# Hybrid attention and SSM layer: later loads, an earlier split and a regrouped frame in the SSM chain

## The chip, the cores and the metric

One core of a Trainium2 chip runs the kernel. The time is that of one execution on the device, in microseconds (us); lower is better. The kernel before took 1496.83 us, the median of three runs (1495.3, 1496.83 and 1497.23).

Five engines run their own instruction streams in order: PE (TensorE, matrix products), DVE (VectorE), ACT (ScalarE), POOL (GpSimd) and SP (which here only issues DMAs). They wait for each other through semaphores. ACT issues DMAs too.

## The reference

One layer over 2048 tokens of width 1024, all in float32. One input projection gives q, k, v, the gate inputs and the SSM input u:

```
h = rms_norm(x); proj = h @ w_in
q, k, v, z_attn, u_ssm, z_ssm, g = split(proj)
attn = windowed_gqa(q, k, v, sink, table) * silu(z_attn)      # 8 heads, window +-128
y = s5_bidirectional(u_ssm, ...)      # 32 groups of 16 channels, 64 complex states,
                                      # a scan over all tokens in both directions
ssm = gelu(y) -> GLU -> * silu(z_ssm)
merged = sigmoid(g_attn) * (attn @ w_a) + sigmoid(g_ssm) * (ssm @ w_s)
out = rms_norm(x + merged @ w_out)
```

The SSM is per group a complex diagonal recurrence x[t] = a x[t-1] + B u[t], y = Re(C x) + D u, forward and backward.

## The kernel before, in words

**Precision.** Each float32 operand of a product is split into a high and a low part (names with h and l at the end: Uh and Ul, Mh and Ml, Hh and Hl). ACT makes the high part, DVE or POOL the low part as the difference. A product is three matmuls: high x high, high x low, low x high.

**Stages.** First u, k and v are projected for the four blocks of 512 tokens. Then come 112 projections of 24 matmuls each (128 columns of w_in, one block of tokens): q, za and zs, then the gate columns g, twice over for two blocks each. Each key of columns serves two projections in a row. Its weights are loaded on SP's queue, their high part is made by ACT (line 163) and their low part by POOL (line 155, four instructions). The result goes from an output bank of PE (three are in turn) to memory through ACT; for za and zs also through DVE (line 401). Beside the projections runs a side chain: first the SSM, then attention, then the preparation of the last stage. GLU, branch and output products follow.

**What sets the order.** The order is written out when the kernel is built. The side chain is a generator. Inside each projection, `turn` is called four times, and each call adds half of a rate to a credit; while the credit is positive, a step of the chain is issued, which costs 1 (half that in attention). RATE2 holds for the SSM and the first part of attention. So a step's instructions stand in each engine's stream behind those of the projections issued until then, whether its engine is by then free or not.

**The SSM chain.** The parameters are computed on DVE beside the first projections. `ssm` then works through 8 frames of 4 groups (half 0 and half 1, two groups each), about 15 steps a frame. In frame i:

- `inject` (line 858) multiplies U, the frame's input, by W into PSUM, and ACT copies it to X; `zmat` (line 821) builds with the output table wo and the input matrix a small matrix Z, which is stored and loaded again as M (`load_m`), 128 wide.
- `rotate` (lines 867 to 870), `scan` (879), `rotate` back, on DVE, half by half.
- `high_h` on ACT and `low_h` on DVE (891) split the states of a half into Hh and Hl; `split_m` (749) gives Mh and Ml.
- `emit(i, half)` (901, 905) on PE adds M x U and ws x H for the half's two groups. ws are the split parts of the table wo.
- For frame i+1, `prep_e` and `prep_w` fill tables on POOL through a list that `slot` empties one by one, `prep_o` the output table wo on DVE (692 to 694), `mats` transposes wt to W on PE (796), `split_u` splits U. `load_u` loads U of frame i+2.

Of the kernel before, what the change touches and what calls it, by code (L numbers as in the profile page):

```python
# [7 lines left out]
F32 = mybir.dt.float32  # L8
# [4 lines left out]
ALU = mybir.AluOpType  # L13
# [10 lines left out]
G, P, C, T = 32, 64, 16, 8  # L24
M = S // T
GB = 4
RATE1 = 1.336
RATEP = 2.6
RATE2 = 1.237
RATE3 = 1.499  # L30
WLAG = 2
WOP = 1
# [5 lines left out]
def kernel(  # L38
# [9 lines left out]
    nc = tc.nc  # L48
    V, A, Q, PE = nc.vector, nc.scalar, nc.gpsimd, nc.tensor
    x = x[0]  # L50
    w_in = w_in[0]
    out = out[0]
# [3 lines left out]
    def scratch(name, shape):  # L56
        if dbg and name in dbg:
            return dbg[name]
        return dram.tile(shape, F32, name=name)

    uS = scratch("uS", [512, T, M])
# [357 lines left out]
    wo_re = prm.tile([128, G, T], F32, name="wo_re")  # L419
    wo_im = prm.tile([128, G, T], F32, name="wo_im")  # L420
# [8 lines left out]
    cc_re = prm.tile([128, G, C], F32, name="cc_re")  # L429
    cc_im = prm.tile([128, G, C], F32, name="cc_im")  # L430
# [238 lines left out]
    def ssm(pool):  # L669
        f, b_ = slice(0, 64), slice(64, 128)  # L670
        st = {}
# [3 lines left out]
        sh = [128, GB, T, C]  # L675

        def bc(t, i, wide):
            return t[:, i * GB:(i + 1) * GB].unsqueeze(3 if wide else 2).to_broadcast(sh)
# [3 lines left out]
        def product(o, p, q, eng):  # L682

            def part(n, a, b, c, d, op, gs):
                if eng is Q:
                    tmp = [pool.tile([128, 2, T, C], F32, tag=f"t{m}", name=f"t{m}") for m in range(2)]
                else:
                    r = rtile().rearrange("p g r m -> p g (r m)")  # L690
                    tmp = [r[:, m].rearrange("p (g j c) -> p g j c", g=GB, c=C) for m in range(2)]
                eng.tensor_tensor(tmp[0], a[:, gs], b[:, gs], ALU.mult)
                eng.tensor_tensor(tmp[1], c[:, gs], d[:, gs], ALU.mult)
                eng.tensor_tensor(o[n][:, gs], tmp[0], tmp[1], op)

            for n, x_ in enumerate(((p[0], q[0], p[1], q[1], ALU.subtract), (p[0], q[1], p[1], q[0], ALU.add))):
                w = 2 if eng is Q else GB
                for g in range(0, o[n].shape[1], w):
                    if eng is Q:
                        work.append(lambda n=n, x_=x_, g=g: part(n, *x_, slice(g, g + w)))  # L700
                    else:
                        part(n, *x_, slice(g, g + w))
# [7 lines left out]
        def slot():  # L710

            count[0] += 1
            if work and (count[0] % 2 == 0 or len(work) > 3):
                work.pop(0)()
            yield

        def rtile():
            return pool.tile([128, 2, 2, M], F32, tag="rt", name="rt")

        def table(o, i, p_re, p_im, q_re, q_im, eng):  # L720
            pr, pi, qr, qi = bc(p_re, i, 1), bc(p_im, i, 1), bc(q_re, i, 0), bc(q_im, i, 0)
            product(o, (pr, pi), (qr, qi), eng)
# [3 lines left out]
            st[i] = {"wt": o}  # L726
            table(o, i, wi_re, wi_im, bb_re, bb_im, eng)

        def prep_o(i, eng=Q):
            raw_o[i] = [pool.tile(sh, F32, tag=f"wo{n}", name=f"wo{n}") for n in range(2)]  # L730
            table(raw_o[i], i, wo_re, wo_im, cc_re, cc_im, eng)

        def prep_e(i, half):

# [8 lines left out]
        def mirror_e(i, half):  # L743
            for n, t in enumerate(ph[i, half]):
                A.activation(t[:, :, 126::-1], t[:, :, 128:255], AF.Copy, scale=1.0 - 2.0 * n)

        def parts(hi, lo, raw):
            A.activation(hi, raw, AF.Copy)
            V.tensor_tensor(lo, raw, hi.bitcast(F32), ALU.subtract)
            return hi, lo  # L750
# [14 lines left out]
        def chan(t, g):  # L765

            return bass.AP(tensor=t.tensor, offset=t.offset + g * C * T * M, ap=[[M, T], [T * M, C], [1, M]])

        def load_u(i, half):
            lo = pool.tile([128, 2, M], F32R, tag=f"U{half}l", name=f"U{half}l", bufs=2)  # L770
            raw = lo.bitcast(F32)
            for j in range(2):
                A.dma_start(out=raw[:, j], in_=chan(uS, i * GB + half * 2 + j))
            raw_u[i, half] = lo, raw

        def split_u(i, half):
            hi = pool.tile([128, 2, M], F32R, tag=f"U{half}h", name=f"U{half}h", bufs=2)
            st[i].setdefault("U", []).append(parts(hi, *raw_u.pop((i, half))))

        def split_m(i):  # L780
            st[i]["M"] = parts(pool.tile([128, GB, 128], F32R, tag="Mh", name="Mh"), *st[i].pop("m"))
# [80 lines left out]
        def rotate(i, half, back):  # L862

            X = st[i]["X"][half][:, :, :, 1:M]
            c, s_ = (t[:, :, 0:M - 1].unsqueeze(2).to_broadcast([128, 2, 2, M - 1]) for t in ph[i, half])
            t = rtile()[:, :, :, 1:M]
            V.tensor_tensor(t, X[:, :, ::-1], s_, ALU.mult)  # L867
            V.tensor_tensor(X, X, c, ALU.mult)
            for r in range(2):
                V.tensor_tensor(X[:, :, r], X[:, :, r], t[:, :, r], ALU.add if r == back else ALU.subtract)  # L870

        def scan(i, half):

            X = st[i]["X"][half]
            for j in range(2):
                g = i * GB + half * 2 + j
                for r in range(2):
                    v = X[:, j, r, 1:M]
                    V.tensor_tensor_scan(v, rho[:, g:g + 1].to_broadcast([128, M - 1]), v, 0.0, ALU.mult, ALU.add)  # L879
# [8 lines left out]
        def low_h(i):  # L888
            H, xs = st[i]["H"]
            for rows, xv in xs:  # L890
                V.tensor_tensor(H[1][rows], xv, H[0][rows].bitcast(F32), ALU.subtract)  # L891
# [21 lines left out]
        def frame(i):  # L913

            nx = i + 1 if i + 1 < NB else None
            nn = i + 2 if i + 2 < NB else None
            ms = mats(nx) if nx else None
            zs = zmat(i)
            inject(i, 0)
            yield from slot()  # L920
            next(zs)
            inject(i, 1)
            yield from slot()
            rotate(i, 0, 0)
            next(zs)
            inject(i, 2)
            yield from slot()
            scan(i, 0)
            next(zs)
            inject(i, 3)  # L930
            if i > 0:
                mirror_e(i, 1)
            yield from slot()
            next(zs, None)
            rotate(i, 0, 1)
            if nx:
                prep_e(nx, 0)
            yield from slot()
            A.dma_start(out=zS[i], in_=st[i].pop("z"))
            if nx:  # L940
                next(ms)
            yield from slot()
            if nx:
                next(ms)
            split_o(i)
            yield from slot()
            load_m(i)
            high_h(i, 0)
            if nx:
                next(ms, None)  # L950
            if nn:
                prep_w(nn)
            yield from slot()
            low_h(i)
            rotate(i, 1, 0)
            yield from slot()
            split_m(i)
            scan(i, 1)
            yield from slot()
            rotate(i, 1, 1)  # L960
            if nx:
                prep_e(nx, 1)
            yield from slot()
            yield from slot()
            yield from emit(i, 0)
            yield from slot()
            high_h(i, 1)
            yield from slot()
            low_h(i)
            if nx:  # L970
                mirror_e(nx, 0)
            yield from slot()
            if nx:
                prep_o(nx, V)
                split_u(nx, 0)
            yield from slot()
            yield from emit(i, 1)
            if nx:
                split_u(nx, 1)
            if nn:  # L980
                load_u(nn, 0)
                load_u(nn, 1)
            st.pop(i)
            yield from slot()

        raw_o, ph = {}, {}
        load_u(0, 0)
        load_u(0, 1)
        prep_w(0, V)
        prep_e(0, 0)  # L990
        prep_e(0, 1)
        drain_work()
        yield
        prep_o(0, V)
        yield
        yield from mats(0)
        split_u(0, 0)
        split_u(0, 1)
        mirror_e(0, 0)
        mirror_e(0, 1)  # L1000
        load_u(1, 0)
        load_u(1, 1)
        prep_w(1)
        yield
        for i in range(NB):
            yield from frame(i)

# [238 lines left out]
    with tc.manual_schedule():  # L1246
# [4 lines left out]
        wo = {}  # L1251
# [80 lines left out]
        for b in range(NBLK):  # L1332
            gen = None
            for i, key in enumerate(wlist):
# [14 lines left out]
                if b == 2 and i == 2:  # L1349
                    pr = add_side(params, RATEP)  # L1350
# [297 lines left out]

        sd = add_side(chain(), RATE2)
        for key in first:  # L1650
# [95 lines left out]
```

## Time and profile before

| | |
|---|---|
| median of the runs | 1496.83 us |
| profiled execution | 1497.58 us |
| its span, first to last instruction | 1495.8 us |
| PE busy | 1411.9 us (94%) |
| DVE busy | 1042.3 us (70%) |
| ACT busy | 659.8 us |
| POOL busy | 636.9 us |
| mean granted clock of PE | 0.981 |

Busy time is the union of an engine's instructions; PE's matmuls overlap, so that one of 128 x 512 lists 0.39 us where the next starts 0.23 us later. A row of a timeline gives start, length, engine, line, operation, result and sources; in brackets stands how long the engine was idle before it and what ended that. The chain of work that ended last is 45% PE and 19% DVE. The SSM frames run from 199 to 660 us, attention from there to about 1045 us.

### The profile page before, as it was taken

What the parts mean: (1) busy time and instruction counts of PE and PEld (TensorE: products, weight loads), DVE (VectorE), ACT (ScalarE), POOL (GpSimd) and SP (SyncE); (2) the same over time, 40 slices, a digit from 0 to 9 for tenths busy, and PEclk for the clock granted to TensorE, in tenths of its full rate; (3) what the DMA queues carried; (4) which work ended last, traced back from release to release, by engine and by line L of the source; (5) the groups of instructions that cost most, each with busy time, mean ns of one, the idle gap of its engine ahead of it and who ended that gap; (6) DMA issues with size and microseconds to landing.
All of it is one profiled execution on the core that took longest, in us unless ns stands there. A gap on an engine that the chain in (4) does not pass through costs nothing.

```text
span 1495.8 us, 19697 instructions
## 1 busy us (share of the span) xinstructions
PE 1411.9 (94%) x6933; PEld 1151.1 (77%) x6933; DVE 1042.3 (70%) x1954; ACT 659.8 (44%) x1213; POOL 636.9 (43%) x683
## 2 busy tenths in 40 slices
PE   7999779899999999899999999999989999999998
PEld 6787567777778777788888888888767887878886
DVE  2427977779788788656999998883678376485442
ACT  6432133433534534535666666664444243243211
POOL 5520187758688787732111111113367054153320
PEclk9999989989999999999999999999999999999999
DMA  8543222322332332455233333334676476375441
GB/s 268 156 105 90 64 81 74 99 92 71 119 106 82 116 106 82 149 170 142 86 95 93 96 95 89 99 99 141 201 210 175 140 185 184 117 186 177 129 120 70
DMA packets 240722, 185.47 MB, mean 124 GB/s; under 512 B 57920, under 2 KB 202432, under 8 KB 240624
## 3 DMA queue, kind: packets, MB, share of 16 engines
q10 hardware_dynamic: 118192, 107.89, 24.5%
q1 hardware_dynamic: 122432, 76.34, 17.1%
q8 instruction: 54, 0.88, 0.2%
q14 instruction: 44, 0.36, 0.1%
HBM read 126.56 MB, written 57.62 MB: 123 GB/s over the span
## 4 chain that ended last, share of the span: by engine, by line
PE 45%; DVE 19%; POOL 7%; DMA 6%; issue 6%; ACT 4%; ACTq 1%; POOLq 0%; DVEq 0%; SPq 0%
PE pj L221 8%; PE pj L220 8%; PE pj L222 8%; PE s L1593 4%; PE s L1592 4%; PE s L1594 4%; POOL wl L155 3%; DMA yt<-yS 2%; PE s L1163 2%; DVE Hl L891 2%; PE s L1110 2%; PE s L1147 2%; DVE pl L1152 1%; PE s L858 1%; DVE X L879 1%
## 5 line engine op out<-in xcount | busy, mean ns | idle before, releaser
L155 POOL TENSOR_TENSOR wl<-raw,wh 128x256 fp32r<-128x256 f32 x380 | 352.9, 959 | 575.1 <-ACT wh L163 443.6
L220 PE MATMUL pj<-hh,wh 128*128 128x512 f32 x976 | 390.7, 400 | 0.0
L221 PE MATMUL pj<-hl,wh 128*128 128x512 f32 x976 | 385.2, 395 | 0.0
L222 PE MATMUL pj<-hh,wl 128*128 128x512 f32 x976 | 385.1, 395 | 0.0
L222 PEld LDWEIGHTS pj<-hh,wl 128*128 128x128 f32 x976 | 185.4, 190 | 40.9
L220 PEld LDWEIGHTS pj<-hh,wh 128*128 128x128 f32 x976 | 186.1, 191 | 33.9
L221 PEld LDWEIGHTS pj<-hl,wh 128*128 128x128 f32 x976 | 185.8, 190 | 34.1
L163 ACT ACTIVATE wh<-raw 128x1024 fp32r<-128x1024 f32 x96 | 100.7, 1051 | 22.0 <-issue 4.4
L1592 PE MATMUL s<-woh,mh 128*128 128x512 f32 x256 | 101.3, 396 | 0.0
L1594 PE MATMUL s<-woh,ml 128*128 128x512 f32 x256 | 101.3, 396 | 0.0
L1593 PE MATMUL s<-wol,mh 128*128 128x512 f32 x256 | 101.3, 396 | 0.0
L1127 ACT ACTIVATE p<-p,sml 128x384 f32<-128x384 f32 (+1 forms) x128 | 75.8, 594 | 16.3 <-DVE sml L1123 16.2
L404 ACT ACTIVATE st<-pj,bg 128x512 f32<-128x512 f32 x64 | 43.8, 685 | 77.7 <-PE pj L222 71.6
L1111 DVE CUSTOM_DVE_ANT_0 p<-s,bias 128x384 f32<-128x384 f32 (+1 forms) x128 | 68.2, 534 | 14.1 <-PE s L1110 13.7
L1636 POOL TENSOR_TENSOR sm<-sm,mhalf 128x1 f32<-128x1 f32 x15 | 8.3, 551 | 160.3 <-DVE sm L1635 123.7
L867 DVE TENSOR_TENSOR rt<-X,es 128x1020 f32<-128x1020 f32 x32 | 43.3, 1353 | 38.1 <-issue 14.3
L1152 DVE TENSOR_TENSOR pl<-s,ph 128x512 fp32r<-128x512 f32 x92 | 62.8, 683 | 4.3 <-ACT ph L1150 2.9
L1110 PE MATMUL s<-kst,qs 128*128 128x384 f32 (+1 forms) x256 | 65.7, 339 | 0.0
L1599 DVE TENSOR_TENSOR xr<-xr,s 128x512 f32<-128x512 f32 x32 | 21.9, 684 | 60.0 <-PE s L1594 60.0
L870 DVE TENSOR_TENSOR X<-X,rt 128x510 f32<-128x510 f32 x64 | 62.1, 1009 | 1.1
L891 DVE TENSOR_TENSOR Hl<-X,Hh 64x1024 fp32r<-64x1024 f32 x32 | 46.1, 1440 | 17.5 <-ACT Hh L886 17.0
L1594 PEld LDWEIGHTS s<-woh,ml 128*128 128x128 f32 x256 | 48.1, 188 | 11.7
(307 smaller groups left out, 3046.1 us busy)
## 6 DMA issues: line engine op xcount, KB each, us to landing
raw<-in_w_in_dram SPq DMA_DIRECT2D x59, 512.0 KB
gS<-st ACTq DMA_DIRECT2D x64, 256.0 KB
gt<-gS ACTq DMA_DIRECT2D x64, 256.0 KB
x<-in_x_dram SPq DMA_DIRECT2D x16, 512.0 KB
raw<-in_w_branch_attn_dram SPq DMA_DIRECT2D x32, 256.0 KB
raw<-in_w_branch_ssm_dram SPq DMA_DIRECT2D x32, 256.0 KB
out_dram<-xr ACTq DMA_DIRECT2D x15, 512.0 KB
xr<-in_x_dram SPq DMA_DIRECT2D x12, 512.0 KB
```

Of the source, the lines that this page charges most:

```text
L155: eng.tensor_tensor(lo[:, ks], r[:, ks], hi[:, ks].bitcast(F32), ALU.subtract)
L163: A.activation(res[0], r, AF.Copy)
L220: PE.matmul(pt, w[0][:, k], r[0][:, k], start=start and k == 0, stop=False)
L221: PE.matmul(pt, w[0][:, k], r[1][:, k], start=False, stop=False)
L222: PE.matmul(pt, w[1][:, k], r[0][:, k], start=False, stop=stop and k == kt - 1)
L891: V.tensor_tensor(H[1][rows], xv, H[0][rows].bitcast(F32), ALU.subtract)
L1110: PE.matmul(pt[:, 0:w], s["qs"][:, h], kst[:, r, kv, k0 * 128:k1 * 128], start=r == 0, stop=r == 1)
L1127: A.activation(p[:, h, 0:w], p[:, h, 0:w], AF.Exp, bias=nm[:, j:j + 1], accum_out=den[:, j:j + 1])
L1152: return lambda: V.tensor_tensor(pl, pt, ph.bitcast(F32), ALU.subtract)
L1592: PE.matmul(pt, mh[k][:, ts_], wo[0, n][:, k], start=k == 0, stop=False)
L1593: PE.matmul(pt, mh[k][:, ts_], wo[1, n][:, k], start=False, stop=False)
L1594: PE.matmul(pt, ml[k][:, ts_], wo[0, n][:, k], start=False, stop=k == KD - 1)
```

## The change

Four things are moved and one number is changed.

- The first loads of U come four steps later and go on SP's queue in place of ACT's. The tables of frame 0 follow them; two more empty steps stand in this prologue.
- In a frame, `split_m` stands ahead of the rotation of half 1, no longer behind it.
- `prep_o` is written as a generator with a stop in the middle. Its first half, with both `split_u` of the next frame, stands in the step that issued nothing, between the last rotation and the first emission. The second half stands where the whole was.
- The loads of U for the frame after next are issued one step later.
- RATE2 goes from 1.237 to 1.28.

```diff
-RATE2 = 1.237
+RATE2 = 1.28
...
-        def prep_o(i, eng=Q):
-            raw_o[i] = [pool.tile(sh, F32, tag=f"wo{n}", name=f"wo{n}") for n in range(2)]
-            table(raw_o[i], i, wo_re, wo_im, cc_re, cc_im, eng)
+        def prep_o(i):
+            o = [pool.tile(sh, F32, tag=f"wo{n}", name=f"wo{n}") for n in range(2)]
+            pr, pi, qr, qi = bc(wo_re, i, 1), bc(wo_im, i, 1), bc(cc_re, i, 0), bc(cc_im, i, 0)
+            for n, (a, b, c, d, op) in enumerate(((pr, qr, pi, qi, ALU.subtract), (pr, qi, pi, qr, ALU.add))):
+                r = rtile().rearrange("p g r m -> p g (r m)")
+                t = [r[:, m].rearrange("p (g j c) -> p g j c", g=GB, c=C) for m in range(2)]
+                V.tensor_tensor(t[0], a, b, ALU.mult)
+                V.tensor_tensor(t[1], c, d, ALU.mult)
+                V.tensor_tensor(o[n], t[0], t[1], op)
+                if n == 0:
+                    yield
+            raw_o[i] = o
...
-        def load_u(i, half):
+        def load_u(i, half, q=A):
...
-                A.dma_start(out=raw[:, j], in_=chan(uS, i * GB + half * 2 + j))
+                q.dma_start(out=raw[:, j], in_=chan(uS, i * GB + half * 2 + j))
...
             low_h(i)
+            split_m(i)
             rotate(i, 1, 0)
             yield from slot()
-            split_m(i)
             scan(i, 1)
             yield from slot()
             rotate(i, 1, 1)
             if nx:
                 prep_e(nx, 1)
             yield from slot()
+            if nx:
+                split_u(nx, 0)
+                split_u(nx, 1)
+                po = prep_o(nx)
+                next(po)
             yield from slot()
             yield from emit(i, 0)
...
             if nx:
-                prep_o(nx, V)
-                split_u(nx, 0)
+                next(po, None)
             yield from slot()
             yield from emit(i, 1)
-            if nx:
-                split_u(nx, 1)
+            st.pop(i)
+            yield from slot()
             if nn:
                 load_u(nn, 0)
                 load_u(nn, 1)
-            st.pop(i)
-            yield from slot()
...
-        load_u(0, 0)
-        load_u(0, 1)
+        for _ in range(4):
+            yield
+        load_u(0, 0, nc.sync)
+        load_u(0, 1, nc.sync)
...
-        prep_o(0, V)
+        yield
+        yield from prep_o(0)
```

Counted in projections issued by then, the first transposes of wt stand on PE at 25.25 (before 23.0), the first inject of frame 0 at 26.75 (24.25), the last emission of frame 7 begins at 85.25 (84.75). Between a frame's first inject and the emission of its half 1 there are 6.5 or 6.75 projections, before 6.75 or 7.0.

On DVE, the end of frame 6 before: the last rotation, the low part of the states of half 1 (Hl), then the output table wo of frame 7 and its U.

```order
L867 TENSOR_TENSOR rt<-X,es 128x4x255
L868 TENSOR_TENSOR X<-X,ec 128x4x255
L870 TENSOR_TENSOR X<-X,rt 128x2x255 x2
L891 TENSOR_TENSOR Hl<-X,Hh 64x1024 x2
L692 TENSOR_TENSOR rt<-wo_re,cc_re 128x512
L693 TENSOR_TENSOR rt<-wo_im,cc_im 128x512
L694 TENSOR_TENSOR wo_5457<-rt 128x512
L692 TENSOR_TENSOR rt<-wo_re,cc_im 128x512
L693 TENSOR_TENSOR rt<-wo_im,cc_re 128x512
L694 TENSOR_TENSOR wo_5458<-rt 128x512
L749 TENSOR_TENSOR U0l<-U0l,U0h 128x512
L749 TENSOR_TENSOR U1l<-U1l,U1h 128x512
```

The same place of DVE's stream now (lines are 10 or 44 higher):

```order
L877 TENSOR_TENSOR rt<-X,es 128x4x255
L878 TENSOR_TENSOR X<-X,ec 128x4x255
L880 TENSOR_TENSOR X<-X,rt 128x2x255 x2
L759 TENSOR_TENSOR U0l<-U0l,U0h 128x512
L759 TENSOR_TENSOR U1l<-U1l,U1h 128x512
L736 TENSOR_TENSOR rt<-wo_re,cc_re 128x512
L737 TENSOR_TENSOR rt<-wo_im,cc_im 128x512
L738 TENSOR_TENSOR wo_5392<-rt 128x512
L901 TENSOR_TENSOR Hl<-X,Hh 64x1024 x2
L736 TENSOR_TENSOR rt<-wo_re,cc_im 128x512
L737 TENSOR_TENSOR rt<-wo_im,cc_re 128x512
L738 TENSOR_TENSOR wo_5393<-rt 128x512
```

Both splits of U and three of the six instructions of the table now stand between the rotation and Hl.

On ACT, the start of the SSM before: the weight split of the second q key, the four loads of U (two rows of two), the evacuation of the first q projection (L396), the first W.

```order
L163 ACTIVATE wh<-raw 128x1024
L773 DMA U0l<-uS 128x1x256 x2
L773 DMA U1l<-uS 128x1x256 x2
L396 ACTIVATE st<-pj 128x512
L799 ACTIVATE Wh<-s_1833 128x512
```

The same place of ACT's stream now, from the same weight split on:

```order
L163 ACTIVATE wh<-raw 128x1024
L396 ACTIVATE st<-pj 128x512
L94 DMA qS<-st 128x512
L396 ACTIVATE st<-pj 128x512
L163 ACTIVATE wh<-raw 128x1024
```

The loads are gone from ACT, and two evacuations and the next weight split come ahead of the first W.

## Rows read from the trace of the kernel before

**Rows 1.** Windows: from:to length, busy us (instructions) of PE, PEld, DVE, ACT, POOL, PEclk, DMA.
```profile
177.00:199.00 22.00, 10.21 (x41) 8.15 (x40) 21.43 (x48) 3.85 (x8) 12.04 (x13) 0.69 0.18 60
...
660.00:1045.00 385.00, 382.17 (x1906) 318.89 (x1905) 313.77 (x903) 236.31 (x562) 71.87 (x92) 1.00 0.37 110
```

**Rows 2.** What PE waited for, 120 to 660 us: total, times, longest.
```profile
PE s L901 <- DVE Ml L749: 11.8, 6, 4.1
...
PE s L858 <- DVE U0l L749: 6.7, 6, 1.6
PE s L796 <- POOL wt L694: 5.4, 1, 5.4
PE s L821 <- ACT wo L760: 4.0, 1, 4.0
PE s L905 <- DVE Hl L891: 3.7, 2, 3.5
```

**Rows 3.** Timeline of ACT, PE, DVE and POOL, the start of the SSM.
```profile
189.17 0.60 ACT L396 ACTIVATE st<-pj 128x512 f32<-128x512 f32 x1 [14.95 <-DMA U1l<-uS]
189.33 1.09 PE L796 MATMUL s<-ident,wt 128*128 128x128 f32 x4 [11.79 <-issue]
...
191.42 0.99 DVE L694 TENSOR_TENSOR wt<-rt 128x512 f32<-128x512 f32 x1
...
198.35 1.06 POOL L694 TENSOR_TENSOR es<-t,t 128x256 f32<-128x256 f32 x1
203.58 2.83 POOL L155 TENSOR_TENSOR wl<-raw,wh 128x256 fp32r<-128x256 f32 x4 [4.16 <-ACT wh L163]
```

**Rows 4.** Timeline of PE behind the wait that ended at 224.02 us.
```profile
224.94 0.63 PE L221 MATMUL pj<-hl,wh 128*128 128x512 f32 x1
225.36 0.63 PE L222 MATMUL pj<-hh,wl 128*128 128x512 f32 x1
...
228.13 0.39 PE L220 MATMUL pj<-hh,wh 128*128 128x512 f32 x1
228.36 0.39 PE L221 MATMUL pj<-hl,wh 128*128 128x512 f32 x1
```

**Rows 5.** Timeline of DVE, frame 4.
```profile
466.32 1.53 DVE L867 TENSOR_TENSOR rt<-X,es 128x1020 f32<-128x1020 f32 x1
...
471.62 1.22 DVE L749 TENSOR_TENSOR Ml<-Ml,Mh 128x512 fp32r<-128x512 f32 x1
...
483.44 2.90 DVE L891 TENSOR_TENSOR Hl<-X,Hh 64x1024 fp32r<-64x1024 f32 x2 [1.13 <-ACT Hh L886]
486.37 1.11 DVE L692 TENSOR_TENSOR rt<-wo_re,cc_re 128x512 f32<-128x512 f32 x1
...
489.81 1.11 DVE L692 TENSOR_TENSOR rt<-wo_re,cc_im 128x512 f32<-128x512 f32 x1
...
492.91 1.21 DVE L749 TENSOR_TENSOR U0l<-U0l,U0h 128x512 fp32r<-128x512 f32 x1
494.04 1.10 DVE L749 TENSOR_TENSOR U1l<-U1l,U1h 128x512 fp32r<-128x512 f32 x1
```

**Rows 6.** Timeline of PE, frame 4: first inject, first use of Hl of half 1.
```profile
438.99 0.28 PE L858 MATMUL s<-U0h,Wh 128*128 128x256 f32 x1
...
486.39 0.39 PE L905 MATMUL s<-Hl,ws0h 128*128 128x256 f32 x1
```

**Rows 7.** Timeline of DVE, frame 6, Hl of half 1.
```profile
592.88 3.47 DVE L891 TENSOR_TENSOR Hl<-X,Hh 64x1024 fp32r<-64x1024 f32 x2 [2.67 <-ACT Hh L886]
```

**Rows 8.** Timeline of POOL and DVE, end of frame 1; POOL's next starts at 334.43.
```profile
322.87 1.07 POOL L694 TENSOR_TENSOR es<-t,t 128x256 f32<-128x256 f32 x1
...
324.41 0.68 DVE L749 TENSOR_TENSOR U0l<-U0l,U0h 128x512 fp32r<-128x512 f32 x1
325.01 0.67 DVE L401 SCALAR_TENSOR_TENSOR st<-th,pj 128x512 f32<-128x512 f32 x1
```

**Rows 9.** Timeline of POOL, frame 4, a weight split.
```profile
485.22 5.16 POOL L155 TENSOR_TENSOR wl<-raw,wh 128x256 fp32r<-128x256 f32 x4
```

More of the change, by code (lines that the diff above doesn't have):

```diff
@@ L998, in ssm @@
         split_u(0, 1)
+        yield
         mirror_e(0, 0)
@@ L1003, in ssm @@
         prep_w(1)
-        yield
+        yield from slot()
         for i in range(NB):
```

## The prediction

> **What bounds the kernel now.** I read the busy times of stretches first. From 660 to 1045 us, where attention runs beside the projections, TensorE is busy 382.17 of 385 us at full clock, so nothing there is to be won or lost by order. In the 22 us from 177 to 199 it is busy 10.21 us at a granted clock of 0.69 [rows 1]. Then the list of what TensorE waited for, cut to 120 to 660 us, the whole SSM phase [rows 2]: six kinds of wait make 43.4 us (the two others there, 0.7 us each, lie before it). Each is a wait for the SSM chain: 11.8 us once before the first transposes [rows 3], and in the list 5.4 us once for POOL's table of frame 1, 11.8 us in six waits for Ml, 6.7 in six for U0l, 3.7 for Hl, 4.0 for wo. To each belongs a slow stretch behind it: after the 5.4 us wait the rows stand 0.42 us apart until 227.5 us and 0.23 us apart from then on, which is half clock for 3.5 us and a loss of about 1.8 us [rows 4]. Seven single waits were of 1.8 us or more (11.8, 5.4, 4.1, 4.0, 3.5, 2.2, 1.8), so I put 7 x 1.8 = 12.6 us to them. The price of the SSM phase is then 43.4 + 12.6 = 56 us over plain TensorE work, and plain work doesn't change. The question is what this 56 becomes.
>
> **The start.** Before, four U loads stand on ACT's queue ahead of the evacuation of the first q projection. They wait for the end of the parameter work on VectorE, and the evacuation waits 14.95 us for them; TensorE stops at 177.54 and goes on at 189.33 [rows 3]. In the changed order the loads are on SP, and TensorE has 2.25 more projections ahead of the first transposes, 54 matmuls of 0.2275 us or 12.3 us. It gets there at about 189.8, when the first half of wt is there; the second is ready at 192.41 [rows 3] and wanted at about 193. This wait is gone. The next one isn't: the weights of projection 26 are split on POOL, and in POOL's order that still stands behind prep_e of frame 0, whose last instruction ends at 199.41 [rows 3]. One quarter of a split takes 0.71 us [rows 3], so the first is there at about 200.2. TensorE wants it at 177.5 + 3 x 5.46 + 1.4 (two groups of transposes and two matmuls) = 195.4. It waits 4.8 us and pays 1.8 us of slow clock: 6.6 us, where before it paid 11.8 + 1.8. SP's queue is held by the U loads until 186.5, but the next weight load behind them waits for POOL's split of projection 26 in any case, which is later. The 5.4 us wait for the table of frame 1 has a quarter of a projection more in front of it and three POOL instructions that begin where they did, near 206; I put nothing to it.
>
> **The parts inside a frame.** Ml comes 5.3 us earlier on VectorE, since the rotation that it now stands ahead of takes that long (in frame 4 the rotation begins at 466.32, Ml at 471.62 [rows 5]). Its waits were 4.1 us at most [rows 2], so they go. The U splits and half of the output table are done a half-frame sooner, so the U0l and wo waits go as well. Nothing of VectorE's work is saved; it is only put elsewhere. What stands behind it there decides.
>
> The place where it is put is called empty since the code of that step issued nothing. It is not empty on VectorE. ACT's Hh there starts when the rotation ends, and the Hl that follows waits only for Hh, 1.13 us [rows 5]: VectorE runs behind the order in which it was issued. In frame 4 Hl ends at 486.34 and TensorE's first use of it is at 486.39 [rows 5, 6], 47.4 us after the frame's first inject at 438.99 [rows 6]. There is no slack at this point. The new order puts five instructions ahead of Hl: U0l, U1l and three of the output table. In frame 4 they cost, from start to start, 494.04 - 492.91 + 1.05 for the splits and 489.81 - 486.37 for the table: 2.18 + 3.44 = 5.6 us [rows 5]. They cover the wait for Hh, 1.13 us in frames 3 to 5 (three such rows) and 2.67 in frame 6 [rows 5, 7]. The faster pace brings the frame's last inject 0.3 us sooner. So Hl is later, against the first inject, by 5.6 - 1.1 - 0.3 = 4.2 us in frame 4, and by 2.6 in frame 6.
>
> TensorE meanwhile gets there sooner. At rate 1.28 it has 6.5 or 6.75 projections between a frame's first inject and the use of Hl, 6.65 on average in frames 2 to 6, where it had 7.0 in frame 4: 0.35 x 5.46 = 1.9 us less. It waits 4.2 + 1.9 = 6.1 us in frame 4 and 4.5 us in a frame like 6; I take 5.2 us and 1.8 us of slow clock behind it, 7.0 us in each of frames 3 to 6. In frames 0 to 2 the projections are in good part za and zs, whose evacuation is also on VectorE, 0.67 us each [rows 8], some five in a frame. Part falls into its idle time; I add 2.5 us, 9.5 us in each. Frame 7 prepares no next frame and has none of it.
>
> **The bounds of that price.** The trace shows the five instructions at both lengths. U0l took 0.68 us at 324.41, when POOL's last had ended at 323.94, and 1.21 us at 492.91 beside POOL [rows 5, 8]. Five short ones are 3.4 us, five of the longest (1.22) 6.1 us. Less the wait for Hh, Hl is 1.9 to 4.7 us later on average. I take the value near the top, because POOL's split of a weight block runs from 485.22 to 490.38 through this place in frame 4 [rows 9], and keep both ends. The Trainium skill (SBUF — State Buffer, section "SBUF: two separate sides") says that a VectorE instruction with two SBUF inputs and a GpSimd instruction that reads SBUF share one pair of ports, which the first to start keeps for its whole length while the other is blocked. The two lengths of U0l agree with it. By that rule the block would cost 3.4 us wherever POOL happens to rest there, which is the first rival below.
>
> **The rest.** Six steps more and the faster rate leave the chain half a projection later at the end of the SSM (85.5 against 85.0) and at the end of attention; about two projections still separate its end from the first GLU block. Nothing is put to it, with 2 us either way. M's split now follows its load by one step less; a load that lands late would hold ACT, and with it the evacuations, by up to 2 us in a frame. I count none.
>
> **The sum.** After: 6.6 + 4 x 7.0 + 3 x 9.5 = 63.1 us in place of 56, which is 7.1 us slower. The profiled execution took 1497.58 us (1.8 us around its span), 0.75 above the median of the runs, 1496.83; from the median this gives 1503.9 us.
>
> **Rivals.**
> - *The block is short.* If POOL rests where the five instructions now stand, they cost 3.4 us; Hl is 1.9 - 0.3 us later, the wait 1.6 + 1.9 = 3.5 us, 5.3 us with its clock. If the za and zs evacuations fall into VectorE's idle time besides, all seven frames pay this: 6.6 + 7 x 5.3 = 43.7 us, 12.3 us less than 56, which gives 1484.5. For it: U0l alone took 0.68 us [rows 8], and the waits for Hl in the list come to only 3.7 us [rows 2]. Against it: POOL's split there in frame 4 [rows 9]. The sign turns where a frame's price falls from 8.1 to 7.1 us, so one microsecond per frame decides.
> - *The step is empty after all.* TensorE never waits for Hl; only the start remains, 6.6 in place of 56: 1448. Against it: two waits for Hl are in the list already, one of 3.5 us [rows 2].
> - *It balances.* Price within 3 us of 56: 1496.8.
> - *The frames with za and zs lose more.* ACT's tanh there can't go on before VectorE has taken the previous one, so a VectorE that is later holds ACT and by it TensorE's output banks: 3 us more in each of three frames, 1513.
>
> **How the numbers follow.** Two runs of this kernel differ by up to 0.13%, so 0.2%, 3 us, counts as no change. Forecast 0.43 (its own range 1499 to 1510), heavier loss 0.10, balance 0.18, short block 0.24, empty step 0.05. Slower is then 0.53, same 0.18, faster 0.29. For 8 in 10 the range takes the short block and the heavier loss in and leaves out the empty step: 1482 to 1514.
>
> **What would show it.** In the changed profile the waits for Ml, U0l and wo are near zero, the wait before the first transposes is gone, and one of 4 to 6 us for POOL's wl stands near 195 us. The list must show waits for Hl at the second emission in seven frames, 4 to 8 us each, some 40 us in all, and the clock low behind each. If those are under 2 us the forecast is wrong, and the time falls well under 1490. If the first wait is not gone, the loads weren't what held the start.

## The result, and the profile after

The changed kernel takes 1516.45 us (median of four runs, 1515.12 to 1516.86), the kernel before 1497.03 in runs beside it: ratio 1.0127, 95% interval 1.011 to 1.0145. That is 19.4 us slower. The forecast was 1503.9 with a range up to 1514, so the sign was right and the size was not; the time lies 2.4 us above the range.

The start did what was forecast. These are the stretches of [rows 1] in the changed kernel; columns are length, then busy time of PE, PEld, DVE, ACT and POOL, the granted clock and the DMA share:

```profile
177.00:199.00 22.00, 19.90 (x92) 16.12 (x90) 21.46 (x48) 6.47 (x11) 12.06 (x14) 1.00 0.28 96
660.00:1045.00 385.00, 377.12 (x1896) 316.65 (x1895) 313.38 (x902) 230.89 (x554) 72.32 (x88) 1.00 0.36 107
```

TensorE is busy 19.90 us where it had 10.21. The second line is a surprise: in attention's window of time TensorE does 5 us less work (377.12 us busy against 382.17). The waits of TensorE from 120 to 660 us, which answer to [rows 2] (total, times, longest):

```profile
PE s L915 <- DVE Hl L901: 32.2, 7, 6.2
PE s L915 <- ACT Hh L896: 10.6, 4, 8.4
PE pj L222 <- POOL wl L155: 5.1, 2, 4.9
PE s L806 <- POOL wt L694: 2.1, 1, 2.1
PE pj L220 <- ACT wh L163: 1.5, 1, 1.5
```

Ml, U0l, wo and the wait before the first transposes [rows 3] are gone. In their place stand Hl and Hh, the two parts of H at a frame's second emission, with 42.8 us together. Frame 4 on VectorE, to be read beside [rows 5], from the start of U0l on:

```profile
492.33 1.10 DVE L759 TENSOR_TENSOR U0l<-U0l,U0h 128x512 fp32r<-128x512 f32 x1
493.36 1.11 DVE L759 TENSOR_TENSOR U1l<-U1l,U1h 128x512 fp32r<-128x512 f32 x1
494.39 1.23 DVE L736 TENSOR_TENSOR rt<-wo_re,cc_re 128x512 f32<-128x512 f32 x1
495.54 0.68 DVE L737 TENSOR_TENSOR rt<-wo_im,cc_im 128x512 f32<-128x512 f32 x1
496.25 1.10 DVE L738 TENSOR_TENSOR wo<-rt 128x512 f32<-128x512 f32 x1
497.28 3.40 DVE L901 TENSOR_TENSOR Hl<-X,Hh 64x1024 fp32r<-64x1024 f32 x2
```

The five instructions take 4.95 us from the first start to the start of Hl, and Hl no longer waits for Hh: that wait lies under them. TensorE at the same place, to be read beside [rows 6]:

```profile
495.05 0.28 PE L915 MATMUL s<-Hh,ws0h 128*128 128x256 f32 x1
500.73 0.58 PE L915 MATMUL s<-Hl,ws0h 128*128 128x256 f32 x1 [5.41 <-DVE Hl L901]
...
502.39 0.63 PE L221 MATMUL pj<-hl,wh 128*128 128x512 f32 x1
502.82 0.63 PE L222 MATMUL pj<-hh,wl 128*128 128x512 f32 x1
...
505.49 0.40 PE L221 MATMUL pj<-hl,wh 128*128 128x512 f32 x1
505.72 0.39 PE L222 MATMUL pj<-hh,wl 128*128 128x512 f32 x1
```

It waits 5.41 us. Behind the wait the rows stand 0.43 us apart, which is half clock as in [rows 4] (the granted clock is 0.50 from 500.5 to 503 us), and 0.23 us apart two to three microseconds later (granted 1.00 from 504.5 us on).

Where the 19 us arose can be read by lining up the same projection in both traces. The changed kernel stands 11.3 us behind at the projection that began at 674.7 us before (the end of the SSM phase), 16.5 us behind at the one of 1028.7 us (the end of attention) and 18.8 us at the last. Of the 11.3, 1.6 us were there at 81 us already, ahead of any changed code. They are one stretch at half clock: up to 42 us the two traces run level, from 46 us on they are 1.6 us apart. The window between, before and after, columns as above:

```profile
43.00:46.40 3.40, 3.40 (x18) 2.78 (x17) 1.27 (x2) 0.69 (x1) 3.40 (x6) 1.00 0.41 105
43.00:46.40 3.40, 3.40 (x11) 2.73 (x10) 1.25 (x2) 0.69 (x1) 3.40 (x6) 0.50 0.27 70
```

Eight of the 17 traces here have this stretch, among them traces of kernels whose code up to there is that of the kernel before (e2, e3); it is not an effect of the change. So the SSM phase cost 9.7 us, attention 5.2, the end 2.3.

### The profile page after: what moved, and what is told of

It is laid out like the page before. It is cut to its first block, busy times and chain, and to the rows that moved or that the text cites. A ratio compares the mean times of both kernels' runs of the same rounds, so it can differ in the third digit from the quotient of the medians.

```text
span 1514.6 us, 19673 instructions
## 1 busy us (share of the span) xinstructions
PE 1415.7 (93%) x6933; PEld 1154.9 (76%) x6933; DVE 1040.5 (69%) x1954; ACT 659.4 (44%) x1213; POOL 641.0 (42%) x683
## 5 line engine op out<-in xcount | busy, mean ns | idle before, releaser
L155 POOL TENSOR_TENSOR wl<-raw,wh 128x256 fp32r<-128x256 f32 x380 | 358.2, 972 | 573.8 <-ACT wh L163 513.8
L1143 ACT ACTIVATE p<-p,sml 128x384 f32<-128x384 f32 (+1 forms) x128 | 75.9, 596 | 14.0 <-DVE sml L1139 13.8
L1166 ACT ACTIVATE ph<-s 128x512 fp32r<-128x512 f32 x92 | 54.4, 591 | 51.2 <-PE s L1163 50.1
L404 ACT ACTIVATE st<-pj,bg 128x512 f32<-128x512 f32 x64 | 43.9, 685 | 74.5 <-PE pj L222 72.7
L1163 PE MATMUL s<-ident,p 128*128 128x128 f32 x368 | 55.6, 276 | 7.3 <-DVE p L1155 6.4
```

The source lines that it names most:

```text
L155: eng.tensor_tensor(lo[:, ks], r[:, ks], hi[:, ks].bitcast(F32), ALU.subtract)
L1143: A.activation(p[:, h, 0:w], p[:, h, 0:w], AF.Exp, bias=nm[:, j:j + 1], accum_out=den[:, j:j + 1])
```

## The experiments

Two theories stood against each other for the SSM. *Block*: the five instructions in the "empty" step hold back Hl, and everything else in the change is worth little or a gain. *Pace*: the rate of 1.28 brings TensorE to its operands too early, wherever they stand. For attention: at RATE3 it issues one and a half of its half steps per turn, six in the four turns of a projection, so each step keeps the quarter of a projection at which it fell when attention began, and the change moved that (*place*); or attention suffers from an SSM that ends later (*backlog*). The place can be set by itself: a little credit for the side chain where the last rate begins.

All ratios are to the kernel before, run beside them on the same chip, with 95% intervals.

| kernel | median us | ratio (interval) |
|---|---|---|
| e1: changed, place moved | 1529.34 | 1.021 (1.0195 to 1.0225) |
| e2: before, place moved | 1535.57 | 1.0242 (1.0222 to 1.0263) |
| e3: before, third pairing | 1498.84 | 1.0001 (0.9988 to 1.0014) |
| e5: changed, place of before | 1511.46 | 1.0081 (1.0062 to 1.0099) |
| e6: start alone | 1502.43 | 1.0025 (1.0012 to 1.0038) |
| e7: M's split alone | 1498.06 | 0.9992 (0.9979 to 1.0004) |
| e8: block alone | 1520.32 | 1.0137 (1.0114 to 1.016) |
| e4: changed, block put back | 1494.6 | 0.9977 (0.9967 to 0.9987) |
| g1: e4, place of before | 1490.41 | 0.994 (0.9925 to 0.9956) |
| g2: g1, U splits first | 1487.39 | 0.992 (0.9908 to 0.9933) |
| g3: g1, M and loads as before | 1489.55 | 0.9928 (0.9914 to 0.9942) |
| g4: g1, third pairing | 1491.53 | 0.9943 (0.9931 to 0.9955) |
| h1: e5, only U splits in the step | 1497.36 | 0.9985 (0.9972 to 0.9999) |
| h2: e5, only the table in the step | 1499.59 | 1.0 (0.9984 to 1.0016) |
| h3: g2, weight split first at the start | 1483.32 | 0.9893 (0.9874 to 0.9911) |

**Attention's place: e1, e2, e3, e5, g4.** The edit is one line, with 0.25 in e1 and e3, 0.5 in e2, 1.75 in e5 and 1.9 in g4:

```
         sd["rate"] = RATE3
+        sd["credit"] += 0.25
```

> The changed kernel, with a quarter of a step added to the side chain's credit at the change to the last rate. Nothing of the SSM's order changes; in attention the steps that share a turn between two output groups are again those of before (a transpose with scores, a transpose with values), where the changed kernel has two transposes and a values step in one turn. Theory 'pairing' (the attention's +5 us come from which steps share a turn): 1511 to 1512 us, TensorE's waits at the values products for VectorE's pl fall from 6.4 us to under 3. Rival 'late chain' (the 5 us come from the SSM ending half a projection later): 1516 us, waits as in the changed kernel.

> The kernel before, with half a step added to the credit at the change to the last rate: its attention gets the changed kernel's pairing, two transposes and a values step in one turn. Theory 'pairing': 1501 to 1503 us, with some 6 us of waits at the values products for pl, 0.4 us each. Rival 'late chain': 1497 us, since the chain ends no later.

> The kernel before with a quarter of a step added there: the third of the three pairings that a rate of one and a half steps per turn allows (a transpose alone; a transpose with two values steps; scores with values; a transpose with both scores). Theory 'pairing': 1497 to 1502 us, as its transposes stand in separate turns but one shares its turn with two values steps. Rival 'late chain': 1497 us.

> The changed kernel with 1.75 steps added to the side chain's credit at the change to the last rate, so that each attention step stands at the same quarter of a projection as in the kernel before (e1 had the same pairs, half a projection off). Theory 'place' (what counts in attention is where in the projection a step is issued, beside the evacuation of the projection's bank): the 5.2 us of attention and up to 2 of the end go, 1509 to 1511.5 us, and no wait at the values products is over 0.5 us. Rival 'backlog' (the chain that left the SSM later is what attention suffers from): 1515 us or more.

My first form of the theory fell with e1. It had the pairs of before, half a projection off, and was by the ratios 12.4 us slower than the changed kernel instead of 5 us faster. e2, the kernel before with the pairs of the changed one, a quarter of a projection off, lost 36 us, all of them in attention (1.9 us behind at the projection of 674.7 us, 38.0 at that of 1028.7). So it isn't the pairs that count but where in the projection they come. e5, with each step at its quarter of before, got back 6.9 us by the ratios (1.0081 against 1.0127, some 4 us either way) and lost 0.6 us in attention (13.2 us behind at the projection of 674.7 us, 13.8 at that of 1028.7). It leaves the SSM as far behind as the changed kernel does, so *backlog* is out. What TensorE and VectorE waited for from 700 to 1030 us says why. L1163 is the values product in e2 and the transpose in the changed kernel, whose values product is L1179; so the 6.4 us that the expectation of e1 put to pl at the values products are waits of the transposes for p, the normalized probabilities. First e2:

```profile
PE s L1163 <- DVE ob L1179: 25.0, 15, 3.2
...
DVE st L401 <- ACT th L400: 20.9, 16, 1.4
```

then the changed kernel:

```profile
PE s L1163 <- DVE p L1155: 6.4, 15, 0.5
...
DVE st L401 <- ACT th L400: 5.1, 16, 1.4
```

and e5:

```profile
PE s L1179 <- DVE pl L1168: 2.6, 11, 0.5
...
DVE st L401 <- ACT th L400: 2.5, 7, 0.5
```

Each za or zs projection ends with a tanh on ACT and a gate on VectorE (st), in both engines' queues among attention's own work. Where attention's exponentials on ACT fall ahead of the tanh, VectorE stands at st, and what is queued behind it (ob, pl) reaches TensorE late. In e2 and e1 this is the main cause. Their waits for the tanh come to 20.9 and 18.6 us, and 15 of the 19 waits of TensorE in e2 start some 2 us behind a wait of 1.1 to 1.4 us of VectorE for the tanh. The order of the projections holds a test too: e2 falls from 1.9 to 39.3 us behind while za and zs run, up to the projection that began at 860.4 us before, and loses nothing more (38.0 at that of 1028.7) beside the g projections, which have no gate on VectorE. Five of its waits, of 1.8 to 3.2 us, have a stretch at half clock behind them besides (granted 0.5).

In the changed kernel it is not the tanh. Its wait for it is 5.1 us in all, against 2.5 us in before and e5, 2.9 in e3 and 2.6 in g4, none of which lost a microsecond in attention, and 3.7 in e4, which lost 5.1 us there. But its 15 waits for p come once in two projections, 0.47 us at most, and go on after the last gate (865.0 us): six of them stand from 888.7 to 988.3 us. One of them, on VectorE, POOL and TensorE:

```profile
766.83 0.75 DVE L1155 TENSOR_SCALAR p<-p,sml 128x384 f32<-128x384 f32 x2
...
769.66 1.46 DVE L1155 TENSOR_SCALAR p<-p,sml 128x384 f32<-128x384 f32 x2
```

```profile
768.67 3.04 POOL L155 TENSOR_TENSOR wl<-raw,wh 128x256 fp32r<-128x256 f32 x4 [17.23 <-ACT wh L163]
```

```profile
771.18 0.33 PE L1163 MATMUL s<-ident,p 128*128 128x128 f32 x1 [0.47 <-DVE p L1155]
```

The normalization of a unit's second pair of heads takes 1.46 us where it overlaps POOL's split of a weight block and 0.75 us elsewhere, and TensorE wants the last head's p just then. Of the 15 waits 14 have POOL's split at that place, and so have all 14 in e4. In before and e5 POOL's split falls on the first pair (mostly 0.98 to 1.49 us), which TensorE wants later, and no such wait stands in either. So what the change moved in attention is the place of VectorE's work beside POOL's. I read this from the traces; no run moved POOL's split by itself.

**One part at a time: e6, e7, e8.** Each is the kernel before with one part. e6 has the prologue of the changed kernel (and a credit of 1 for the same place in attention). The edits of e7 and e8:

```
 e7:         low_h(i)
            +split_m(i)
             rotate(i, 1, 0)
             yield from slot()
            -split_m(i)
 e8:         yield from slot()            (the step behind prep_e(nx, 1))
            +split_u(nx, 0); split_u(nx, 1); po = prep_o(nx); next(po)
             ...
            -prep_o(nx, V); split_u(nx, 0); ... split_u(nx, 1)
            +next(po, None)
```

> The kernel before with the later start alone (loads of U four steps later and on SP, the yields around them), at rate 1.237, attention's steps at the same quarters of a projection as before. Theory 'start is worth its wait' (the sum of the prediction: 6.6 us in place of 13.6): 1490 us. Rival 'given back' (the chain is some projection later in every frame, the frames' waits grow by what the start saved): 1496 to 1499 us.

> The kernel before with M's split ahead of the rotation and nothing else. Theory 'M's wait is its own' (the 11.8 us of waits for Ml and two slow stretches behind them go, nothing takes their place): 1497 - 11.8 - 3.6 = 1482 us. Rival 'no slack behind it' (the rotation, the second Hh and Hl come 1 us later per frame, and TensorE waits there instead): 1490 to 1495 us.

> The kernel before with the U splits and half of the output table in the empty step and nothing else: rate 1.237, start and M as before. Theory 'block' (VectorE's five instructions push Hl and ACT's Hh): Hl and Hh waits of some 3.8 us in frames 3 to 6 and 6.3 in 0 to 2 with 1.8 us of slow clock each, 46.7 us, against 10.7 us of U0l and wo with 3.6 of clock and 5.5 for Hl before: 1497 + 27 = 1524 us. Rival 'pace' (the wait for Hl came from the rate of 1.28, which brings TensorE 1.9 us sooner): 2 us in each frame, no slow clock, 1497 + 14 - 14 = 1497 us.

The block alone costs 20.5 us at the old rate (1.37% of 1497); *pace* is out as the main cause. M's early split alone is worth nothing that can be measured: the rival was nearer. Its wait list, 120 to 700 us:

```profile
PE s L858 <- DVE U0l L749: 9.7, 7, 2.1
PE pj L220 <- DVE st L401: 6.0, 2, 5.6
PE s L796 <- POOL wt L694: 5.4, 1, 5.4
PE s L905 <- DVE Hl L891: 5.4, 6, 2.0
PE s L821 <- ACT wo L760: 4.9, 1, 4.9
```

Ml's 11.8 us are gone; U0l has 3.0 more, st 6.0 that were not there, Hl 1.7 and wo 0.9 more, together 11.6, and smaller new ones come to 2.5. The start alone is 3.8 us slower, outside both expectations. It stands 17.0 us ahead of before at the projection of 969 us and 6.0 us behind at the end. The chain has six steps more at the old rate, and its last values product comes two projections later than in before, counted in the trace (126.75 against 124.75). The GLU behind it then waits for what the end of the chain prepares (1040 to 1100 us, 12.5 us of waits in all where before has 6.6):

```profile
PE pj L220 <- ACT ta L1534: 6.0, 2, 4.7
PE s L220 <- ACT sh L1537: 2.1, 1, 2.1
PE pj L220 <- ACT wh L163: 1.7, 1, 1.7
PE pj L220 <- ACT gh L1457: 1.5, 1, 1.5
```

So the later start needs the rate of 1.28: with it and without the block, in g3, the ratio is 0.9928 against 1.0025 here. Whether the rate would pay alone no run shows.

**Without the block: e4, g1, g2, g3, g4.** e4 is the changed kernel with the block's five instructions back where they were; g1 adds attention's place of before (credit 1.75, as in g2, g3 and h1 to h3). g2 changes the order there:

```
             if nx:
+                split_u(nx, 0); split_u(nx, 1)
                 for _ in prep_o(nx): pass
-                split_u(nx, 0)
             yield from slot()
             yield from emit(i, 1)
-            if nx: split_u(nx, 1)
```

g3 is g1 with M's split and the U loads as in before.

> The changed kernel with the U splits and both halves of the output table back behind the second low part of H, as in the kernel before; the later start, M's early split, the later U loads and the rate of 1.28 stay, and so does the changed pairing in attention. Theory 'block' (the five instructions ahead of Hl on VectorE cost what the SSM lost): the waits for Hl fall from 32 to some 13 us (7 x 1.9, since the faster pace brings TensorE 1.9 us sooner), those for Hh from 10.6 to about 1, and U0l and wo are back with 6.7 and 4.0: start 6.6 + 13 + 1 + 10.7 = 31 us in place of 56, and the time is 1497 - 25 + 7 for attention and the end = 1479 us. Rival 'pace' (TensorE waits for the chain at rate 1.28 wherever the block stands): the waits only change their names, 1510 to 1517 us.

> The kernel of e4 (the changed kernel without the block in the empty step) with attention's steps at the quarters of a projection where they stand in the kernel before. Theory 'place': as from the changed kernel to e5, 5 us less than e4: ratio to before 0.993, about 1490 us, no wait at the values products over 0.6 us. Rival 'backlog': as e4, ratio 0.998.

> g1 with both U splits right behind the second low part of H, ahead of the output table (before: table, then the two splits). Theory 'the last of the row waits' (TensorE wants U0l first, wo some 20 us later): the waits for U0l, 6.2 us, go and none comes for wo: 4 to 6 us under g1, about 1485 us. Rival 'wo next': wo, 2.4 us later, is waited for by as much in each frame, and g2 is within 2 us of g1 or above it.

> g1 with M's split behind the rotation and the U loads a step earlier again, so that it is the kernel before with the later start and the rate of 1.28. Theory 'VectorE's queue' (what M's early split takes from one wait it gives to the next, as in e7): within 3 us of g1. Rival 'M's wait is its own' at this pace: 10 to 15 us above g1.

> g1 with attention's steps in the third pairing, at the quarters that e3 had. There the waits for pl and p fell from 2.4 to 0.5 us without a gain in time. Theory: within 2 us of g1. Rival: 2 to 4 us under g1, since the wait for the gate's store, which took e3's gain, stands elsewhere at this pace.

Without the block the same change is faster than before: 0.6% with attention's place set, 0.2% without. *Pace*, which had 1510 to 1517 us for e4, is out. g1 against e5 is the block alone: 1.0081 - 0.994 is 1.41%, 21 us, as in e8. For e4 I had set 31 us of price against 56 and left the slow clock out of the 31. Its waits make 36 us (11.7 for Hl, 5.7 Hh, 6.2 U0l, 4.9 wl and smaller ones), and six of them are of 1.8 us or more: 47 in place of 31. At the end of the SSM e4 stands 10.8 us ahead of before; at that of attention it has 5.7 left and at the end 3.4. g1, whose trace is that of its fastest run, has 9.8, 9.7 and 11.5. g3 within 2 us of g1 says again that M's split is worth nothing here. g2 is 3 us under g1, between its two expectations, and the two intervals overlap; its waits for U0l are gone. g4 is as g1.

**Inside the block: h1, h2.** h1 has in the step only the two lines `split_u(nx, 0)` and `split_u(nx, 1)`, h2 only `po = prep_o(nx)` and `next(po)`; the rest stands as in g1.

> The kernel of e5 with the U splits alone in the empty step; both halves of the output table stand behind the second low part of H. Against g1 (nothing in the step, 1490.4 us). Theory 'length less cover' (ahead of Hl only what outlasts the 1.1 us wait for Hh counts): two splits of 1.1 us less 1.1 are 1.1 us in each of seven frames, 7 to 8 us, less 6.4 us of U0l waits that go: 1492 us, Hl and Hh waits together 25 us. Rival 'full length' (VectorE is late all along, so nothing covers): 2.2 x 7 = 15 less 6.4, 1499 us.

> The kernel of e5 with half of the output table alone in the empty step; the U splits stand where they did before the change. Theory 'length less cover': 3.4 less 1.1 us in seven frames, 16 us, less 1 us of waits for wo, U0l stays with 6.4: 1505 us. Rival 'full length': 3.4 x 7 = 24, 1513 us. Rival 'only the splits hurt' (they wait on ACT behind the gate's store): 1491 us.

h1 is 0.45% above g1, 6.7 us; h2 0.60%, 9.0 us; both at once 21. The parts don't add up (by 5 us, with intervals that leave some 5 us either way), and the waits for Hl in frame 4 show why. In order g1, h1, h2 and e5:

```profile
483.42 0.39 PE L915 MATMUL s<-Hl,ws0h 128*128 128x256 f32 x1 [1.18 <-DVE Hl L901]
```

```profile
488.48 0.58 PE L915 MATMUL s<-Hl,ws0h 128*128 128x256 f32 x1 [2.54 <-DVE Hl L901]
```

```profile
491.96 0.58 PE L915 MATMUL s<-Hl,ws0h 128*128 128x256 f32 x1 [3.14 <-DVE Hl L901]
```

```profile
499.38 0.58 PE L915 MATMUL s<-Hl,ws0h 128*128 128x256 f32 x1 [5.41 <-DVE Hl L901]
```

In the same frame VectorE's Hl of g1 waits for Hh:

```profile
480.46 2.90 DVE L901 TENSOR_TENSOR Hl<-X,Hh 64x1024 fp32r<-64x1024 f32 x2 [1.13 <-ACT Hh L896]
```

From first start to the start of Hl, what stands ahead takes 2.06 us in h1, 3.10 in h2 and 4.94 in e5. Less the cover of 1.13 and added to the 1.18 of g1 this gives waits of 2.11, 3.15 and 4.99 us; measured are 2.54, 3.14 and 5.41. In frames 3, 5 and 6 the same working comes out 0.3 to 0.8 us under the measured waits for Hl. So the rule of the prediction, length less the covered wait, holds there to within a microsecond, part by part. The cover is spent once: in each of frames 3 to 6 what the block adds to the wait exceeds what its two parts add by 0.4 to 0.9 us. The whole time doesn't bear the rule out: h1 is 5 us above *length less cover* and within 2 us of *full length*, h2 5 us under *length less cover* and 13 under *full length*. For h1 the difference to *length less cover* lies partly in its longer single waits: 2.34 to 3.06 us for Hl in frames 3 to 6, with slow rows behind, where the waits of g1 for Hl there are 0.96 to 1.49; and Hh of frame 1 waits 2.2 us more than in g1. That *only the splits hurt*, ACT's queue being in their way, is out.

**The start once more: h3.** In g2's prologue the second half of prep_e goes behind the output table:

```
         prep_e(0, 0)
-        prep_e(0, 1)
         drain_work()
         ...
         yield
+        prep_e(0, 1)
+        drain_work()
         yield from mats(0)
```

> g2 with the second half of prep_e of frame 0 behind the first weight split on POOL (6.2 us of POOL's work that stood ahead of it). Theory 'POOL's order holds the start' (the 5.0 us wait for wl near 197 us and 1.8 us of slow clock): the wait goes, 6 to 7 us under g2, about 1481 us. Rival 'given back' (the chain's first frames become late by as much, as in e7): within 2 us of g2.

1483.32 us, 0.27% under g2 by the ratios, 4 us, while the intervals overlap a little. The 5.0 us wait for wl is gone; U0l, wo and wt near it wait 2.2, 1.3 and 0.7 us more, so between the two expectations. It is the fastest kernel here: 1.07% under before and, by the ratios, 2.3% under the changed one.

## Why the prediction was right in its sign and wrong in its size

**The start** held. The wait for wl was forecast with 4.8 us near 195; it was 4.89, from 196.90 on. The wait for frame 1's table, to which nothing was put, fell from 5.4 to 2.1 and no further.

**What goes** held: Ml, U0l and wo are out of the list.

**The waits for Hl** held as a sum: seven frames of 5.2 and 7.7 us made 43.9, measured were 42.8 for Hl and Hh. Their make-up was off in both directions. In frames 3 to 6 the wait is 5.4 to 6.9 us where 5.2 stood (the prediction's own 6.1 in three frames and 4.5 in one average 5.7): without the block 1.2 us remain (g1), where 1.9 were put to the pace, and the block adds 4.2 in frame 4 as forecast and more in frames 3, 5 and 6. In frames 0 to 2 it is 3.6, 12.0 and 3.1 where 7.7 stood. That the sum came so near is luck in part. Frame 1 carries the loss, by a path that I had only as a rival and there by the tanh: the store of a gate stands on ACT ahead of Hh, and waits for VectorE's st, which stands behind the block. VectorE, then ACT, frame 1 of the changed kernel:

```profile
317.01 0.69 DVE L738 TENSOR_TENSOR wo<-rt 128x512 f32<-128x512 f32 x1
317.62 0.68 DVE L401 SCALAR_TENSOR_TENSOR st<-th,pj 128x512 f32<-128x512 f32 x1
```

```profile
318.33 0.33 ACTq L94 DMA_DIRECT2D zsS<-st  x1
318.70 1.06 ACT L896 ACTIVATE Hh<-X 64x1024 fp32r<-64x1024 f32 x1 [8.73 <-DVE st L401]
```

**The slow clock** was sized about right. Eight waits with 1.8 us each were forecast after the change, against seven before; from 120 to 660 us the granted clock falls to 0.5 in nine stretches, against seven. (One wait more in the trace of before has such a length, 1.91 us for Ml at 583.54, with no slow stretch behind it.) The SSM phase came out at +9.7 us and not +7.1 by the waits: they grew by 8 us where the sum has 5.3, mostly through two to which nothing was put, the 2.1 us for frame 1's table and 1.5 for a weight split on ACT. That leaves under 2 us for the clock, as in the sum.

**The short block**, the first rival, is real in one frame: in frame 2 the U splits ran at 0.68 us each while POOL rested (371.6 to 378.1 us), and frame 2 has the smallest wait. In frames 3 to 6 POOL was at work beside most of the five, as [rows 9] said. The rule of the Trainium skill (SBUF — State Buffer, section "SBUF: two separate sides"), that such VectorE instructions and POOL's share a pair of ports, agrees with the trace: 0.68 us there, 1.10 to 1.22 beside POOL.

**The step that failed** is the one on the rest: attention and the end "half a projection later", "Nothing is put to it, with 2 us either way". It measured 7.5 us, 5.2 in attention and 2.3 behind it. The 5.2 are the place: with it set back attention loses 0.6 us (e5), and without the block 0.1 (g1) where e4 loses 5.1; by the ratios the whole gain is 6.9 us (e5) and 5.5 (e4 to g1), some 3 to 4 us either way. Whether the 2.3 behind it come from the place stays open: e5's trace still has 1.8 of them, g1's none. The step saw that the chain comes half a projection later and asked only whether it still ends in time. It didn't ask what each attention step then falls beside; the trace shows POOL's weight split beside the normalization that TensorE wants first. TensorE's 382 busy of 385 us [rows 1] I read as "nothing to be lost by order"; such a share says that there is little to gain, and nothing of what there is to lose. Of the rest of the miss, 2.6 us are the SSM's and 1.6 the half-clock stretch at 43 us, which is in no term of the sum.

By the ratios the change then adds up so: the block +21 us (g1 to e5), attention's place +7 (e5 to changed), and start, pace, loads and M together -9 (before to g1), +19 in all, each term with 2 to 4 us either way.

## What to carry to other kernels

A free step in the order in which work was issued is no free time on the engine: look at what is queued behind it there and how much of a wait it covers, and count that cover once. A change of issue rate or step count in one phase moves the place of every later phase that runs in lockstep with something, so fix that place before judging the change. When such a phase slows down, look behind each wait for what made the releaser late: the longest list of waits on another engine (here for the tanh) need not be the cause. An edit that takes a wait away is tested alone and with its partners: M's split gave its 11.8 us to other waits, and the later start pays only with the faster rate.

## What was not expected of the hardware

By the place of the same instructions alone attention took 36 us more, on 354 (e2), with no single wait over 3.2 us. VectorE's normalization of two heads, with one large input, took 1.46 us beside POOL's weight split and 0.75 without it (changed kernel, 766 to 771 us). A wait of 1.18 us left the matmuls behind it 0.23 us apart at a granted clock of 1.00 (g1, frame 4); one of 2.54 us was followed by rows at half speed, with 0.50 granted (h1: the 256-column product took 0.41 us, in g1 0.28). And the early part of the program, ahead of any change, has in eight of 17 traces a stretch at half clock from 42 or 43 us on, which costs some 1.5 us; what sets it off no run shows.
